# A gated retention and SGU layer on one core: u's projection in half-block products, the sums of the activations formed beside the retention, the mixing spread behind gate pairs

## The chip, the cores and the metric

The kernel runs on one core of one Trainium2 chip. The metric is the device time of one execution in microseconds, as the median of several runs. All inputs and the output are float32 in HBM; the kernel is written by hand in the Tile layer, which tracks dependences, allocates the buffers of its pools and orders each engine's instructions by a schedule made when the program is built.

## The reference, cut to what matters

SEQ = 512, D_MODEL = 1024, chunks of 128, 4 retention heads (dk 128, dv 256), 4 SGU groups, D_FF = 2816.

```
h    = rmsnorm(x, g_pre_mix)
q, k, v, g, u, sv, a_ret, a_sgu = split(h @ w_in)        # 512 512 1024 1024 1024 1024 1024 1024
y_ret = (layernorm(retention_fwd(q,k,v) + retention_bwd(q,k,v)) * silu(g)) @ w_ret_o
mixed = w_spatial (128 positions x 128, per group) @ layernorm(gelu(sv)) + b_spatial
y_sgu = (gelu(u) * mixed) @ w_sgu_o
x1   = x + rmsnorm((sigmoid(a_ret) * y_ret + sigmoid(a_sgu) * y_sgu) @ w_out, g_post_mix)
y    = x1 + rmsnorm(conv_gated_mlp(rmsnorm(x1, g_pre_ffn)), g_post_ffn)
```

## The kernel before, in words

**Products.** Every float32 matrix is split into a high part in float32r and the rest (`split`, L69 to L78: ScalarE copies the high part, VectorE subtracts), and a product is three matmuls, high x high, high x low, low x high (`mm3`, L164 to L166). Activations lie transposed, [channel, position], with 512 positions as the moving side; a weight block is 128 x 1024.

**Weights.** All weights are one array `wall` of 146 blocks. `w_get` (L150) hands out the next unit in order and prepares the following ones as far as slots allow: SyncE loads a block into one of 5 `raw` buffers (L106, pieces of block 0 at L119), and the split goes into 9 `w4` slots (two for a whole block, one for a half-block form). The order in which units are listed (L87 to L96) is the order of use.

**Order of the work.** (1) 18 matmuls on zeros (L201) while the first loads run; x transposed is loaded block by block (`load_x` L184, six `tmp` buffers), scaled by g_pre_mix and split (`x_low`, L193), and q and k are accumulated over the eight channel blocks in all 8 PSUM banks (L211, then `mm3`). (2) Decays, rotary tables, the iota tiles `dd` and `xx` (L303, in the big pool `blk` of 70 tiles) and their clips (L309). (3) For each of four heads the retention (`prep`, `k_rows`, `scores`, `states`, `values`), interleaved with `t_group` (L386 to L388), which projects v, sv and g. (4) `u` in eight whole blocks (`f_block`, L543), each followed by Gelu; between them `x_forms` (L558) loads x again and forms, on VectorE, the sums S1, S2, S4, and `x_form3` (L578) replaces the second half of xh and xl by a difference. (5) The spatial mixing of all eight channel blocks in one go (L674), evacuated by VectorE (L682, L690). (6) Eight gate pairs (`gated_pair`, L697), four with w_ret_o and four with w_sgu_o: a `Pair` (L589) computes two 128-channel blocks of a gate's projection in seven half-block products instead of eight (Strassen's scheme as Winograd arranged it), each of 12 matmuls of 256 columns (L603), on weight sums (T1 to T4, `w_form` L127) and activation sums; `part1` is four products, `part2` one, `part3` two with the sigmoid, and the two `f_block`s of the pair stand between part1 and part2 and between part2 and part3. (7) w_out (`Down`, L727), norms, the convolved MLP, w_down. Down takes all 8 PSUM banks.

**Names that the prediction uses.** T1, T2, T3, T4 and B11, B21, B22 are the seven weight forms. L637, L640 and L641 evacuate part3, L714 multiplies a block by its gate on VectorE, L715 adds the retention's share on GpSimd, L745 to L747 are Down's matmuls.

Of the kernel before, what the change touches and what calls it, by code (L numbers as in the profile page):

```python
# [24 lines left out]
DV = 256  # L25
EPS = 1e-6
NW = 146
GATE0, GATE1 = 40, 72
LOOK = 4
NBLK = 70  # L30
WARM = 18
# [9 lines left out]
def tile_block(ctx: ExitStack, tc, xT, x, wall, par, cs, decay, wsp, bsp, gpost, gffn, out):  # L41
# [25 lines left out]
    def const(n, shape):  # L67
        return sb.tile(list(shape), F32, tag=n, bufs=1, name=n)

    def copy(o, i):  # L70
        nc.scalar.activation(out=o, in_=i, func=AF.Copy)  # L71
# [12 lines left out]
    units = []  # L84
    i = 0
    while i < NW:
        if GATE0 <= i < GATE1:  # L87
            units += [("B11", i), ("B21", i), ("T1", i), ("T2", i), ("blk", i + 2), ("T3", i), ("blk", i + 3)]
            units += [("T4", i), ("B22", i)]
            i += 4  # L90
        else:
            units.append(("blk", i))
            i += 1
# [72 lines left out]
        nc.tensor.matmul(o, al, bh, start=False, stop=stop)  # L166


    part = const("part", [P, NPAR])
    nc.scalar.dma_start(part, par)  # L170

# [3 lines left out]
    nc.vector.memset(warm, 0.0)  # L175
    w16 = warm.bitcast(mybir.dt.bfloat16)
    copy(wact, warm[:, 0:16])

    def col(i):
        return part[:, i : i + 1]  # L180
# [116 lines left out]
    v.tensor_mul(sinr, sinr, rbc)  # L297


    (dp, dn), (xp, xn) = halves("dd"), halves("xx")  # L300

    def iota(o, pattern, base, mult):
        nc.gpsimd.iota(  # L303
            o, pattern=pattern, base=base, channel_multiplier=mult,
            allow_small_or_imprecise_dtypes=True,
        )

    def clip(o, i, op):
        v.tensor_scalar(out=o, in0=i, scalar1=0.0, scalar2=None, op0=op)  # L309

    iota(dp.rearrange("p (i n) -> p i n", i=2), [[-P, 2], [1, 256]], 0, -1)
    clip(dn, dp, ALU.min)
    clip(dp, dp, ALU.max)
    iota(xp, [[1, S]], -255, 0)
    iota(xn, [[1, S]], -256, 0)
    clip(xp, xp, ALU.max)
    clip(xn, xn, ALU.min)
    ze = const("ze", [P, NT])
# [175 lines left out]
    def sv_norm():  # L494
        for t in range(NT):
            for q in range(2):
                z = svz[t, q]
                v.tensor_scalar(
                    out=z, in0=z, scalar1=smv[:, t, 0:1], scalar2=srstd[:, t : t + 1],
                    op0=ALU.subtract, op1=ALU.mult,  # L500
                )
# [20 lines left out]
        transposed([o_sb[t, nh] for t in range(NT)], ogh, ogl)  # L522


    for h in range(H):
        gen = t_group()
        k_rows(h)
        sm = scores(h)
        acc = next(gen)
        st = states(h)  # L530
        next(gen)
        if h + 1 < H:
            prep(h + 1)
        values(h, sm, st)
        for _ in gen:
            pass
        (v_evac, sv_evac, sv_evac, g_evac)[h](acc, (1, 0, 1, 0)[h])
    for acc in t_group():
        pass
    sv_norm()  # L540
    g_evac(acc, 1)

    def f_block(ah, al, n):  # L543

        wh, wl = w_get()
        o = ps()
        for k in range(n):
            c = slice(k * P, (k + 1) * P)
            mm3(o, wh[:, c], wl[:, c], ah[k], al[k], k == 0, k == n - 1)
        return o  # L550

    T0, T1 = slice(0, 256), slice(256, 512)
    forms = {n: [] for n in ("S1", "S2", "S4")}

    def x_forms(k):  # L558

        a, b = tmp("xa"), tmp("xb")  # L560
        for t, j in ((a, k), (b, k + 4)):
            nc.sync.dma_start(t, xT[j])
            nc.scalar.activation(out=t, in_=t, func=AF.Copy, scale=col(PRE + j))
        s_ = tmp("xs")
        v.tensor_sub(s_[:, T0], a[:, T1], b[:, T1])
        v.tensor_sub(s_[:, T1], s_[:, T0], a[:, T0])
        h_, l_ = blk(F32R, "sh"), blk(F32R, "sl")
        split(h_, l_, s_)
        forms["S1"].append((h_[:, T0], l_[:, T0]))
        forms["S2"].append((h_[:, T1], l_[:, T1]))  # L570
        if k % 2 == 0:
            forms["s4"] = blk(F32R, "sh"), blk(F32R, "sl")
        h_, l_ = (t[:, (T0, T1)[k % 2]] for t in forms["s4"])
        v.tensor_add(s_[:, T0], b[:, T0], s_[:, T1])
        split(h_, l_, s_[:, T0])
        forms["S4"].append((h_, l_))

    def x_form3(k):  # L578

        a = tmp("xa")  # L580
        nc.sync.dma_start(a, xT[k])
        v.tensor_sub(a[:, T0], a[:, T0], a[:, T1])
        nc.scalar.activation(out=xh[k][:, T1], in_=a[:, T0], func=AF.Copy, scale=col(PRE + k))
        v.scalar_tensor_tensor(
            out=xl[k][:, T1], in0=a[:, T0], scalar=col(PRE + k), in1=as32(xh[k][:, T1]),
            op0=ALU.mult, op1=ALU.subtract,
        )

    class Pair:  # L589


        def __init__(self):
            self.b = [ps() for _ in range(3)]
            self.t = [tmp("p0"), tmp("p1")]

        def product(self, b, act, first):
            wh, wl = w_get()
            o = self.b[b][:, T0]
            for k in range(4):
                c = slice(k * P, (k + 1) * P)  # L600
                h_, l_ = act(k)
                for n, (w_, a_) in enumerate(((wh, h_), (wh, l_), (wl, h_))):
                    nc.tensor.matmul(  # L603
                        o, w_[:, c], a_, start=first and k == n == 0, stop=k == 3 and n == 2,
                        skip_group_check=True,
                    )
            return o
# [26 lines left out]
        def part3(self, func):  # L634
            c0, c1 = self.t
            o = self.product(0, self.x(4, T1), False)
            v.tensor_mul(c0[:, T1], o, rbc[:, T1])  # L637
            nc.scalar.activation(out=c0, in_=c0, func=func)
            o = self.product(2, self.s("S4"), False)
            v.tensor_sub(c1[:, T0], o, c1[:, T0])  # L640
            v.tensor_mul(c1, c1, rbc)  # L641
            nc.scalar.activation(out=c1, in_=c1, func=func)
            return c0, c1


    nc.sync.dma_start(wst, wsp)
# [3 lines left out]
    nc.tensor.matmul(rw, ones, wst, start=True, stop=True)  # L650
    rws = blk(n="rws")
    copy(rws, rw)
    uT = []
    for j in range(KD):
        o = f_block(xh, xl, KD)
        t = blk(n="u")
        v.tensor_mul(t, o, rbc)
        nc.scalar.activation(out=t, in_=t, func=AF.Gelu_apprx_tanh)
        uT.append(t)
        if j % 2:  # L660
            x_forms(j // 2)
    for k in range(4):
        x_form3(k)
    yh, yl = [], []
    for j in range(KD):
        gs = slice((j // 2) * P, (j // 2 + 1) * P)
        add = tmp("add", (P, P))
        v.scalar_tensor_tensor(
            out=add, in0=rws[:, gs], scalar=col(LNB + j), in1=bst[:, gs],
            op0=ALU.mult, op1=ALU.add,  # L670
        )
        o = ps()
        for t in range(NT):
            nc.tensor.matmul(  # L674
                o[:, t * P : (t + 1) * P],
                svz[t, j // 4][:, (j % 4) * P : (j % 4 + 1) * P],
                wst[:, gs],
                start=True,
                stop=True,
            )  # L680
        m = tmp("mix")
        v.scalar_tensor_tensor(  # L682
            out=m.rearrange("p (t q) -> p t q", t=NT),
            in0=o.rearrange("p (t q) -> p t q", t=NT),
            scalar=col(LNG + j),
            in1=add[:, None, :].to_broadcast([P, NT, P]),
            op0=ALU.mult,
            op1=ALU.add,
        )
        v.tensor_mul(uT[j], m, uT[j])  # L690
        h_, l_ = blk(F32R, "yh"), blk(F32R, "yl")
        split(h_, l_, uT[j])
        yh.append(h_)
        yl.append(l_)


    def gated_pair(ah, al):  # L697
        p = Pair()
        p.part1()
        o = [f_block(ah, al, KD)]  # L700
        p.part2()
# [296 lines left out]
```

## Time and profile before

| | |
|---|---|
| median of 3 runs | 857.89 us (857.30 to 858.48) |
| the profiled execution | 853.59 us, its span 851.8 us, granted TensorE clock 0.997 |
| busy in the span | PE 840.8, PEld 717.2, DVE 525.5, ACT 366.2, POOL 57.8 us |
| instructions | 10890, of them 4300 matmuls |
| HBM | 88.19 MB read, 2.10 MB written, 106 GB/s over the span |

The page's engines are PE (TensorE's matmuls), PEld (its weight loads), DVE (VectorE), ACT (ScalarE), POOL (GpSimd) and SP (SyncE, which issues nearly all loads here). A line number is that of the kernel before. "idle before, releaser" names what ended the time in which an engine stood still. Matmuls are pipelined, so a row's busy time of one is longer than the distance from one start to the next; the distance is what a stage's length shows. Times in microseconds count from the start of the span.

### The profile page before, as it was taken

The numbers are of one execution on the slowest core, as the hardware profiler recorded it, in microseconds if no ns is written. First come the engines' busy times: TensorE is split into PE (matmuls) and PEld (weight loads), VectorE is DVE, ScalarE is ACT, GpSimd is POOL, SyncE is SP. The second block draws the span as 40 slices with busy tenths as digits, with TensorE's granted clock in tenths as the row PEclk, the third lists the DMA queues.
The fourth block names the chain that finished last, engine by engine and source line by source line (L and its number), as shares of the span: only waits on it lengthen the run. The fifth ranks groups of instructions, "written<-read, shape, count | busy, mean of one in ns | idle before, by whom it ended". The sixth has DMA issues, their size and how long they took to land.

```text
span 851.8 us, 10890 instructions
## 1 busy us (share of the span) xinstructions
PE 840.8 (99%) x4300; PEld 717.2 (84%) x4300; DVE 525.5 (62%) x805; ACT 366.2 (43%) x575; POOL 57.8 (7%) x67
## 2 busy tenths in 40 slices
PE   8999999999999999999989999999999999999997
PEld 6888888888889899999978898888888888888885
DVE  6378888863669966667755766666666666322304
ACT  5534445543644533344534664444444444212201
POOL 0000000100000021123210100000000000000000
PEclk9999999999999999999999999999999999999998
DMA  9623212222332332323457032223222322222202
GB/s 337 232 91 115 80 53 75 75 86 95 129 107 67 128 121 99 100 98 101 131 168 246 1 103 99 96 98 99 100 98 99 99 99 98 91 93 90 74 1 99
DMA packets 28851, 90.99 MB, mean 107 GB/s; under 512 B 3264, under 2 KB 3904, under 8 KB 28800
## 3 DMA queue, kind: packets, MB, share of 16 engines
q1 hardware_dynamic: 27648, 87.96, 30.5%
q0 software_dynamic: 432, 1.32, 0.6%
q10 hardware_dynamic: 720, 1.02, 0.3%
q8 instruction: 33, 0.54, 0.3%
q14 instruction: 18, 0.15, 0.1%
HBM read 88.19 MB, written 2.10 MB: 106 GB/s over the span
## 4 chain that ended last, share of the span: by engine, by line
PE 97%; DVE 1%; DMA 1%; ACT 0%; POOL 0%; SPq 0%; issue 0%; POOLq 0%; DVEq 0%; ACTq 0%
PE ps L164 17%; PE ps L166 17%; PE ps L165 17%; PE ps L603 9%; PE ps L745 6%; PE ps L747 6%; PE ps L746 6%; PE ps L386 5%; PE ps L387 5%; PE ps L388 5%; PE ps L674 1%; DMA raw<-wall 1%; PE ps L211 1%; PE ps L511 0%; PE ps L807 0%; DVE wl L78 0%
## 5 line engine op out<-in xcount | busy, mean ns | idle before, releaser
L78 DVE TENSOR_TENSOR wl<-raw,wh 128x1024 fp32r<-128x1024 f32 (+1 forms) x139 | 162.1, 1177 | 188.0 <-PE ps L165 100.1
L71 ACT ACTIVATE wh<-raw 128x1024 fp32r<-128x1024 f32 (+2 forms) x141 | 137.2, 985 | 103.8 <-PE ps L747 40.9
L166 PE MATMUL ps<-h2h,wl 128*128 128x512 f32 (+1 forms) x384 | 142.3, 371 | 0.0
L165 PE MATMUL ps<-h2l,wh 128*128 128x512 f32 (+1 forms) x384 | 142.2, 371 | 0.0
L164 PE MATMUL ps<-h2h,wh 128*128 128x512 f32 (+1 forms) x384 | 142.2, 372 | 0.0
L166 PEld LDWEIGHTS ps<-h2h,wl 128*128 128x128 f32 x384 | 72.3, 188 | 12.6
L165 PEld LDWEIGHTS ps<-h2l,wh 128*128 128x128 f32 x384 | 72.3, 188 | 12.5
L164 PEld LDWEIGHTS ps<-h2h,wh 128*128 128x128 f32 x384 | 72.1, 188 | 12.5 <-ACT h2h L811 0.3
L386 PE MATMUL ps<-wh,xh 128*128 128x512 f32 x192 | 75.0, 391 | 0.0
L387 PE MATMUL ps<-wl,xh 128*128 128x512 f32 x192 | 74.9, 390 | 0.0
L388 PE MATMUL ps<-wh,xl 128*128 128x512 f32 x192 | 74.8, 390 | 0.0
L745 PE MATMUL ps<-wh,fh 128*128 128x512 f32 x176 | 68.5, 389 | 0.0
L746 PE MATMUL ps<-wl,fh 128*128 128x512 f32 x176 | 68.5, 389 | 0.0
L747 PE MATMUL ps<-wh,fl 128*128 128x512 f32 x176 | 68.5, 389 | 0.0
L854 ACT ACTIVATE cv<-ps,part 128x512 f32<-128x512 f32 x44 | 34.3, 780 | 76.3 <-PE ps L166 76.3
L71 ACT ACTIVATE wf<-raw 128x512 fp32r<-128x512 f32 x56 | 33.7, 625 | 59.4 <-PE ps L165 28.1
L603 PE MATMUL ps<-xh,wf 128*128 128x256 f32 x256 | 49.1, 281 | 0.0
L78 DVE TENSOR_TENSOR wf<-raw,wf 128x512 fp32r<-128x512 f32 x56 | 40.9, 742 | 12.0 <-ACT wf L71 11.5
L164 PE MATMUL ps<-xh,wh 128*128 128x512 f32 x120 | 46.8, 390 | 0.0
L166 PE MATMUL ps<-xh,wl 128*128 128x512 f32 x120 | 46.7, 389 | 0.0
L165 PE MATMUL ps<-xl,wh 128*128 128x512 f32 x120 | 46.7, 389 | 0.0
L388 PEld LDWEIGHTS ps<-wh,xl 128*128 128x128 f32 x192 | 36.1, 188 | 7.6
(232 smaller groups left out, 1545.6 us busy)
## 6 DMA issues: line engine op xcount, KB each, us to landing
raw<-wall SPq DMA_DIRECT2D x145, 512.0 KB, 3.3
x<-x SPq DMA_DIRECT2D x16, 256.0 KB, 6.0
xT<-xT SPq DMA_DIRECT2D x8, 256.0 KB, 5.6
xa<-xT SPq DMA_DIRECT2D x8, 256.0 KB, 2.9
xb<-xT SPq DMA_DIRECT2D x4, 256.0 KB, 3.6
out<-z SPq DMA_DIRECT2D x4, 256.0 KB, 2.0
out<-z ACTq DMA_DIRECT2D x3, 256.0 KB, 2.0
cs<-cs SPq DMA_DIRECT2D x2, 256.0 KB, 4.8
```

What stands on the lines that cost most here:

```text
L71: nc.scalar.activation(out=o, in_=i, func=AF.Copy)
L78: nc.vector.tensor_sub(lo, src, as32(hi))
L164: nc.tensor.matmul(o, ah, bh, start=start, stop=False)
L165: nc.tensor.matmul(o, ah, bl, start=False, stop=False)
L166: nc.tensor.matmul(o, al, bh, start=False, stop=stop)
L386: nc.tensor.matmul(acc[t], xh[k][:, c], wh[:, f], start=k == 0, stop=False)
L387: nc.tensor.matmul(acc[t], xh[k][:, c], wl[:, f], start=False, stop=False)
L388: nc.tensor.matmul(acc[t], xl[k][:, c], wh[:, f], start=False, stop=k == KD - 1)
L603: nc.tensor.matmul(o, w_[:, c], a_, start=first and k == n == 0, stop=k == 3 and n == 2, skip_group_check=True,)
L745: nc.tensor.matmul(o, ah, bh, start=k == 0, stop=False)
L746: nc.tensor.matmul(o, ah, bl, start=False, stop=False)
L747: nc.tensor.matmul(o, al, bh, start=False, stop=k == self.nk - 1)
```

## The change

- **u in pairs.** The eight blocks of u (32 to 39 of `wall`) become four `Pair`s with seven products each, with no whole block between them. The host lays u's weights out in quarters as it does those of the gates. part3 of a pair comes behind part1 of the next pair; the last one's behind part1 of the first gate pair.
- **Sums beside the retention.** `x_forms(h)` runs inside head h, in tiles of `blk` instead of `tmp`, its three sums on GpSimd (L536 of the changed kernel) instead of VectorE; the splits of its results follow one head later (`x_form_parts`). `x_form3` stays ahead of u's first pair; its difference is on GpSimd too, and its tile from `blk`.
- **The iota tiles** move from four `blk` tiles into two `raw` buffers that are allocated at the very top, ahead of the first weight block, and are filled there.
- **Mixing.** The eight channel blocks' mixing stands behind the first four gate pairs, two behind each.
- **Gate pairs.** part3 stands in the middle of the pair's second `f_block` (after four of its eight steps) instead of behind it; its two weight forms are taken ahead of the block.

```diff
-GATE0, GATE1 = 40, 72
+U0, GATE0, GATE1 = 32, 40, 72
...
-        if GATE0 <= i < GATE1:
-            units += [("B11", i), ("B21", i), ("T1", i), ("T2", i), ("blk", i + 2), ("T3", i), ("blk", i + 3)]
-            units += [("T4", i), ("B22", i)]
+        pair = [(f, i) for f in ("B11", "B21", "T1", "T2", "T3", "T4", "B22")]
+        if U0 <= i < GATE0:
+            units += pair
+            i += 2
+        elif GATE0 <= i < GATE1:
+            units += pair[:4] + [("blk", i + 2)] + pair[4:] + [("blk", i + 3)]
             i += 4
...
+    (dp, dn), (xp, xn) = ((t[:, :S], t[:, S:]) for t in (raw_tile(), raw_tile()))
+
     part = const("part", [P, NPAR])
     nc.scalar.dma_start(part, par)
...
+    iota(dp.rearrange("p (i n) -> p i n", i=2), [[-P, 2], [1, 256]], 0, -1)
+    iota(xp, [[1, S]], -255, 0)
+    iota(xn, [[1, S]], -256, 0)
...
-    (dp, dn), (xp, xn) = halves("dd"), halves("xx")
...
+    def x_forms(k):
+
+        a, b = blk(n="xa"), blk(n="xb")
+        for t, j in ((a, k), (b, k + 4)):
+            nc.sync.dma_start(t, xT[j])
+            nc.scalar.activation(out=t, in_=t, func=AF.Copy, scale=col(PRE + j))
+        s_ = blk(n="xs")
+        g_op(s_[:, T0], a[:, T1], b[:, T1], ALU.subtract)
+        g_op(s_[:, T1], s_[:, T0], a[:, T0], ALU.subtract)
+        g_op(b[:, T1], b[:, T0], s_[:, T1], ALU.add)
+        return s_, b[:, T1]
...
+    def x_form3(k):
+
+        a = blk(n="xa")
+        nc.sync.dma_start(a, xT[k])
+        g_op(a[:, T0], a[:, T0], a[:, T1], ALU.subtract)
+        nc.scalar.activation(out=xh[k][:, T1], in_=a[:, T0], func=AF.Copy, scale=col(PRE + k))
+        v.scalar_tensor_tensor(
+            out=xl[k][:, T1], in0=a[:, T0], scalar=col(PRE + k), in1=as32(xh[k][:, T1]),
+            op0=ALU.mult, op1=ALU.subtract,
+        )
...
         if h + 1 < H:
             prep(h + 1)
+        if h:
+            x_form_parts(h - 1, *xf)
+        xf = x_forms(h)
         values(h, sm, st)
...
-    def f_block(ah, al, n):
+    def f_block(ah, al, n, between=None):
...
+            if between and k == n // 2:
+                between()
...
-    uT = []
-    for j in range(KD):
-        o = f_block(xh, xl, KD)
-        t = blk(n="u")
-        v.tensor_mul(t, o, rbc)
-        nc.scalar.activation(out=t, in_=t, func=AF.Gelu_apprx_tanh)
-        uT.append(t)
-        if j % 2:
-            x_forms(j // 2)
     for k in range(4):
         x_form3(k)
+    uT, late = [], None
+    for j in range(KD // 2):
+        p = Pair(AF.Gelu_apprx_tanh, lambda: blk(n="u"))
+        p.part1()
+        if late:
+            late.part3()
+        p.part2()
+        late = p
+        uT += p.t
     yh, yl = [], []
-    for j in range(KD):
+
+    def mix(j):
...
-    def gated_pair(ah, al):
-        p = Pair()
+    def gated_pair(ah, al, late=None):
+        p = Pair(AF.Sigmoid, lambda: tmp("sig"))
         p.part1()
+        if late:
+            late.part3()
         o = [f_block(ah, al, KD)]
         p.part2()
-        o.append(f_block(ah, al, KD))
-        return zip(o, p.part3(AF.Sigmoid))
+        o.append(f_block(ah, al, KD, p.part3))
+        return zip(o, p.t)
...
     for j in range(KD // 2):
-        for o, t in gated_pair(ogh, ogl):
+        for o, t in gated_pair(ogh, ogl, late if j == 0 else None):
             b = blk(n="r")
             v.tensor_mul(b, o, t)
             r.append(b)
+        mix(2 * j)
+        mix(2 * j + 1)
...
-        _parts(u, 8, P),
+        _two(u).reshape(8, P, 1024),
```

More of the change, by code (lines that the diff above doesn't have):

```diff
@@ L177, in tile_block, with iota @@
     copy(wact, warm[:, 0:16])
+    def iota(o, pattern, base, mult):
+        nc.gpsimd.iota(
+            o, pattern=pattern, base=base, channel_multiplier=mult,
+            allow_small_or_imprecise_dtypes=True,
+        )
+    iota(dp.rearrange("p (i n) -> p i n", i=2), [[-P, 2], [1, 256]], 0, -1)
+    iota(xp, [[1, S]], -255, 0)
+    iota(xn, [[1, S]], -256, 0)
     def col(i):
@@ L297, in tile_block @@
     v.tensor_mul(sinr, sinr, rbc)
-    (dp, dn), (xp, xn) = halves("dd"), halves("xx")
[L302 to L306, printed above, removed]
     def clip(o, i, op):
         v.tensor_scalar(out=o, in0=i, scalar1=0.0, scalar2=None, op0=op)
-    iota(dp.rearrange("p (i n) -> p i n", i=2), [[-P, 2], [1, 256]], 0, -1)
     clip(dn, dp, ALU.min)
     clip(dp, dp, ALU.max)
-    iota(xp, [[1, S]], -255, 0)
-    iota(xn, [[1, S]], -256, 0)
     clip(xp, xp, ALU.max)
@@ L522, in g_evac, with g_op, x_form_parts @@
         transposed([o_sb[t, nh] for t in range(NT)], ogh, ogl)
+    T0, T1 = slice(0, 256), slice(256, 512)
+    forms = {n: [] for n in ("S1", "S2", "S4")}
+    def g_op(o, a, b, op):
+        nc.gpsimd.tensor_tensor(out=o, in0=a, in1=b, op=op)
+    def x_forms(k):
[8 more added lines that the diff above has]
+        return s_, b[:, T1]
+    def x_form_parts(k, s_, s4):
+        h_, l_ = blk(F32R, "sh"), blk(F32R, "sl")
+        split(h_, l_, s_)
+        forms["S1"].append((h_[:, T0], l_[:, T0]))
+        forms["S2"].append((h_[:, T1], l_[:, T1]))
+        if k % 2 == 0:
+            forms["s4"] = blk(F32R, "sh"), blk(F32R, "sl")
+        h_, l_ = (t[:, (T0, T1)[k % 2]] for t in forms["s4"])
+        split(h_, l_, s4)
+        forms["S4"].append((h_, l_))
+    def x_form3(k):
[6 more added lines that the diff above has]
+            op0=ALU.mult, op1=ALU.subtract,
+        )
     for h in range(H):
@@ L539, in tile_block @@
         pass
+    x_form_parts(3, *xf)
     sv_norm()
     g_evac(acc, 1)
-    def f_block(ah, al, n):
+    def f_block(ah, al, n, between=None):
         wh, wl = w_get()
@@ L550, in f_block, with __init__, product @@
         return o
[L555 to L587, printed above, removed]
     class Pair:
-        def __init__(self):
+        def __init__(self, func, alloc):
+            self.func, self.t = func, [alloc(), alloc()]
             self.b = [ps() for _ in range(3)]
-            self.t = [tmp("p0"), tmp("p1")]
-        def product(self, b, act, first):
-            wh, wl = w_get()
+        def product(self, b, act, first, w=None):
+            wh, wl = w or w_get()
             o = self.b[b][:, T0]
@@ L632, in part2, with part3 @@
             v.tensor_sub(c1[:, T1], self.b[2][:, T0], c1[:, T1])
-        def part3(self, func):
+            self.w = w_get(), w_get()
+        def part3(self):
             c0, c1 = self.t
-            o = self.product(0, self.x(4, T1), False)
+            o = self.product(0, self.x(4, T1), False, self.w[0])
             v.tensor_mul(c0[:, T1], o, rbc[:, T1])
-            nc.scalar.activation(out=c0, in_=c0, func=func)
-            o = self.product(2, self.s("S4"), False)
+            nc.scalar.activation(out=c0, in_=c0, func=self.func)
+            o = self.product(2, self.s("S4"), False, self.w[1])
             v.tensor_sub(c1[:, T0], o, c1[:, T0])
             v.tensor_mul(c1, c1, rbc)
-            nc.scalar.activation(out=c1, in_=c1, func=func)
-            return c0, c1
+            nc.scalar.activation(out=c1, in_=c1, func=self.func)
     nc.sync.dma_start(wst, wsp)
```

## The prediction

> **What bounds the kernel now.** I read the page first: the row of busy times, then the chain of work that ended last.
>
> ```profile
> PE 840.8 (99%) x4300; PEld 717.2 (84%) x4300; DVE 525.5 (62%) x805; ACT 366.2 (43%) x575; POOL 57.8 (7%) x67
> ...
> PE 97%; DVE 1%; DMA 1%; ACT 0%; POOL 0%; SPq 0%; issue 0%; POOLq 0%; DVEq 0%; ACTq 0%
> ```
>
> TensorE has work for 99% of 851.8 us and is 97% of the chain. So a change gains by taking matmul time away or by closing one of TensorE's few gaps, and it loses wherever it opens a gap. The view of waits, filtered to TensorE, lists the gaps.
>
> ```profile
> PE ps L745 <- DVE p L714: 2.3, 1, 2.3
> PE ps L211 <- ACT wh L71: 1.3, 2, 0.9
> ```
>
> One is in the middle (w_out waits for VectorE), the other at the start (the first projection waits for its weights). Stage lengths come from the chain in order of time (start, us, what).
>
> ```profile
> 217.70 0.23 PE ps L164
> ...
> 261.25 7.14 PE ps L674 x64
> ...
> 369.84 8.48 PE ps L603 x72
> ```
>
> u's projection runs from 217.70 to 261.25, which is 43.55 us for 192 matmuls of 512 columns (227 ns each). A matmul of 256 columns in the gates' pairs costs 8.48/72 = 118 ns. The mixing is 64 instructions in 7.14 us without a gap.
>
> **The change part by part.**
>
> *u in pairs.* Four pairs of seven products of twelve matmuls are 336 matmuls: 336 x 0.118 = 39.6 us in place of 43.55. **-4.0 us**, if TensorE is fed.
>
> *Mixing behind the gate pairs.* The same 64 instructions stand in four groups of 16, one behind each of the first four gate pairs. A gate pair in a window (length, then busy time of PE, PEld, DVE, ACT, POOL), and the mixing's evacuation among the groups by form:
>
> ```profile
> 307.40:328.20 20.80, 20.80 (x134) 18.89 (x133) 12.76 (x20) 8.29 (x14) 3.01 (x2) 1.00 0.31 102
> ```
>
> ```profile
> L682 DVE SCALAR_TENSOR_TENSOR mix<-ps,part,add 128x512 f32<-128x512 f32 x8 | 5.9, 741 | 0.0
> ```
>
> VectorE has 8.0 us free in each, and two mixes bring it two such operations, a multiply and a split each, some 4.2 us. **0**, hidden by the pair's matmuls; without that cover a group costs up to two evacuations, 1.5 us, and four of them 6.
>
> *part3 inside the second block.* Now the last pair is evacuated while four of the block's eight steps still run. The chain, where w_out begins before the change:
>
> ```profile
> 434.36 1.22 DVE wl L78
> ...
> 441.55 0.61 DVE p L714
> 442.20 0.50 PE ps L745
> ```
>
> TensorE wants all eight PSUM banks for w_out; the eighth is the last block's, which the second L714 frees only at 442.2, 7.8 us after the chain turns to the pair's evacuation, because its sigmoid comes after the block. Afterwards T4 ends 4.1 us before the block does (twelve matmuls of 118 ns and twelve of 227), so even the whole 7.8 us would free the bank 3.7 us after the block, and TensorE wants it 21 matmuls (4.8 us) after. The 2.3 us go; it takes a chain longer by 1.1 us to bring some back. What is late next is the last mh, wanted 60 matmuls (13.7 us) after the block. **-2.3 us**.
>
> *The iota tiles in two raw buffers, allocated first.* This is the part the diff hides. In the program order of the changed kernel, SyncE's queue starts with all eight xT loads and wst, and only then come the three pieces of the first weight block; before, one xT load stood ahead of them. The seventh xT load needs the first of six tmp buffers back, so SyncE waits for VectorE's first x_low, and the weights wait behind it. VectorE's order has all eight x_low and two clips ahead of the cast of the first piece. The timeline of before, the rows of the tile xT and its loads, and the row of the clips:
>
> ```profile
> 0.73 0.39 SPq L186 DMA_DIRECT2D xT<-xT  x1
> ...
> 1.04 3.78 PE L201 MATMUL ps<-warm 128*128 128x256 bf16 x18 [1.04 <-DVE warm L175]
> ...
> 4.09 0.72 ACT L188 ACTIVATE xh<-xT,part 128x512 fp32r<-128x512 f32 x1 [1.42 <-DMA part<-par]
> 4.29 0.23 DVE L120 CAST wh<-raw 128x128 fp32r<-128x128 f32 x1 [3.31 <-DMA raw<-wall]
> ...
> 4.84 0.75 DVE L194 SCALAR_TENSOR_TENSOR xl<-xT,part,xh 128x512 fp32r<-128x512 f32 x1 [0.32 <-ACT xh L188]
> ...
> 12.27 0.39 PE L164 MATMUL ps<-xh,wh 128*128 128x512 f32 x1
> ```
>
> ```profile
> L194 DVE SCALAR_TENSOR_TENSOR xl<-xT,part,xh x8: 744/748/752, 4.8 to 30.5; 128x512 fp32r<-128x512 f32 x8
> ...
> DMA to landing us min/median/max: 3.1/5.6/7.6
> ```
>
> ```profile
> L309 DVE TENSOR_SCALAR dd<-dd x2: 420/424/429, 52.1 to 52.6; 128x512 f32<-128x512 f32 x2
> ```
>
> From 4.84 VectorE has 8 x 0.75 + 2 x 0.42 + 0.23 = 7.1 us, so its cast ends at 11.9, or 11.1 if neighbours overlap as they do elsewhere; I take 11.5. The landing gives about the same: the first piece is issued near 7.2 (seventh x load after 5.6, eighth after 6.3, then wst) and lands at 10.4 by the shortest time of the row, 12.3 by a 5 us one. The 24 matmuls of k = 0 then need 24 x 0.227 = 5.45 us and end at 16.95; before, the next k starts at 12.27. That is **+4.7 us** (3.6 to 5.9 by the two landings).
>
> TensorE then stands still from 4.8 to 11.5. Windows of the end of before (stretch, length, busy per engine, granted clock, DMA) show what rest does to the clock:
>
> ```profile
> 845.00:846.00 1.00, 0.43 (x2) 0.01 (x1) 0.00 (x0) 0.47 (x1) 0.00 (x0) 1.00 0.00 0
> ...
> 847.00:848.00 1.00, 0.00 (x0) 0.00 (x0) 0.87 (x3) 0.00 (x0) 0.11 (x1) 0.77 0.00 0
> 848.00:849.00 1.00, 0.00 (x0) 0.00 (x0) 0.69 (x2) 0.00 (x0) 0.00 (x0) 0.50 0.23 88
> ```
>
> Two to three us after the last matmul the clock is half. Climbing out is seen in the warm-up row: 18 matmuls of 256 columns took 3.78 us, 210 ns each against 118 later, so 1.66 us were lost. Bounds are 0 (the clock holds) and the whole 3.78; I take the row's own, **+1.7 us**.
>
> The Trainium skill ("TensorE: Matmul & The Clock Gate", Part 1) says that the array drops to half clock after an idle window of about 3.4 us and climbs back only after about 3.4 us of sustained work, the windows running free. An estimate from that page alone is a loss of 1.7 to 3.4 us here, so the sum would be up to 1.7 us higher; the trace's rows agree with its lower end.
>
> *x_form3 on GpSimd.* The third-form halves of x must be there for T3 of pair 0, which TensorE reaches 64 matmuls (7.6 us) after u begins; its last reader stands 83 matmuls (9.8 us) after. In GpSimd's order the four subtractions stand behind T4 of pair 1, two before and two after T2 of pair 2. GpSimd's and VectorE's groups by form:
>
> ```profile
> L140 POOL TENSOR_TENSOR raw<-raw,raw 128x512 f32<-128x512 f32 x8 | 14.2, 1777 | 116.8 <-ACT sh L71 47.4 <-DMA raw<-wall 39.8 <-DVE raw L138 29.6
> ...
> L142 POOL TENSOR_TENSOR raw<-raw,raw 128x512 f32<-128x512 f32 x8 | 10.7, 1342 | 57.1 <-DVE wf L78 38.3 <-DMA raw<-wall 18.9
> ```
>
> ```profile
> L78 DVE TENSOR_TENSOR wf<-raw,wf 128x512 fp32r<-128x512 f32 x56 | 40.9, 742 | 12.0 <-ACT wf L71 11.5
> ...
> L139 DVE TENSOR_TENSOR raw<-raw,raw 128x512 f32<-128x512 f32 x8 | 9.9, 1233 | 0.1
> L641 DVE TENSOR_TENSOR p<-p,rbc 128x512 f32<-128x512 f32 x8 | 6.3, 790 | 0.0
> ...
> L138 DVE TENSOR_TENSOR raw<-raw 128x512 f32<-128x512 f32 x8 | 5.5, 683 | 0.0
> ...
> L640 DVE TENSOR_TENSOR p<-ps,p 128x256 f32<-128x256 f32 x8 | 3.4, 421 | 5.0 <-PE ps L603 5.0
> ```
>
> T4 of pair 1 waits for the split of T2, whose slot is freed when the second product ends (2.8 us) and which stands behind the transposes' copies: about 4.5 us. Then 1.3 (L142), two subtractions at half that, T2 at 1.8 (L140) and two more: 4.5 + 1.3 + 1.3 + 1.8 + 1.3 = 10.2, and ScalarE's and VectorE's halves, with a weight split between them, take until 11.9. TensorE stands for 11.9 - 9.8 = **+2.0 us**. Bounds: 0 (it is on time), 4.5 (a subtraction of 256 columns as slow as 512). No row shows one on GpSimd; half of L142 is nearest.
>
> Behind ScalarE's xh of that form stands its copy of pair 0's T2, which frees the bank that T3 accumulates into; it is late by less than the halves, so it adds nothing.
>
> *The sums beside the retention.* Per head they add to VectorE two splits (0.7 + 0.4) and to GpSimd three subtractions. One head before:
>
> ```profile
> 73.20:102.65 29.45, 29.45 (x163) 25.59 (x161) 25.64 (x44) 13.78 (x21) 1.21 (x2) 1.00 0.22 72
> ```
>
> GpSimd's work is not free to VectorE. The timeline of GpSimd, of VectorE where the two meet, and of VectorE where they don't:
>
> ```profile
> 437.38 1.29 POOL L715 TENSOR_TENSOR p<-p,r 128x512 f32<-128x512 f32 x1 [16.21 <-DVE p L714]
> ```
>
> ```profile
> 437.67 1.55 DVE L641 TENSOR_TENSOR p<-p,rbc 128x512 f32<-128x512 f32 x1
> ```
>
> ```profile
> 311.17 0.68 DVE L641 TENSOR_TENSOR p<-p,rbc 128x512 f32<-128x512 f32 x1
> ```
>
> A VectorE operation on two SBUF tensors begun beside GpSimd's ended 0.55 us after it: 1.55 us, not 0.68. The Trainium skill ("GPSIMD Engine Reference", 1. Specifications) says the same, that GpSimd shares its SBUF interface with such VectorE instructions; it speaks against moving sums to GpSimd while VectorE is full. So a head's VectorE work rises from 25.6 to 25.6 + 1.1 + some 2.0 = 28.7 of 29.45 us. I cost this at **0**: TensorE's next weight blocks are split up to three ahead, and scores and states are needed a block or more after they are made. If that cover is gone, it is up to 3.1 us in each of three heads. Three raw buffers for weights in place of five hold: a block lasts TensorE 5.5 us and takes 3.3 to land, by the page's row of its 145 loads.
>
> ```profile
> raw<-wall SPq DMA_DIRECT2D x145, 512.0 KB, 3.3
> ```
>
> *VectorE in u's stage.* A pair costs it 7 x 0.742 + 0.683 (the other sum, L138) + 1.233 + 5 x 0.42 + 0.79 = 10.0 us of busy rows (some 1 us of it overlap) against TensorE's 9.9. Its splits may lag, since the slots give a pair's weights seven products of lead; I cost it **0**, bounds 0 and 4 us.
>
> **Sum.** 4.7 + 1.7 - 4.0 + 2.0 - 2.3 = +2.1 us. The profiled execution (853.59 us, span 851.8) would become 855.7; it ran 4.3 us below the median of the runs shown, so I add the difference to the median: 857.89 + 2.1 = **860.0**. A difference under 0.2% (1.7 us) can't be told from none.
>
> **Rivals.**
> - *VectorE becomes the bound* in u's stage and the retention. For: 10.0 against 9.9 us, 28.7 of 29.45. Against: no gap in the retention before, seven products of lead. Half of the bounds, (9.3 + 4)/2 less the lag the lead absorbs (2), is +4.6: 864.6 us.
> - *The third-form halves are on time.* For: 64 matmuls, four of pair 1's among them, stand ahead of T3. Against: GpSimd's rows. 2.0 us less: 858.0, no change.
> - *The start is not lost* (the other side). If first pieces and their cast come as early as before, the 6.4 us vanish and 853.6 is left. It decides where the start costs under 2.6 us, a first matmul before 7.7. For: the loads ahead of the pieces are only 2.3 MB. Against: SyncE's and VectorE's orders, which are fixed when built.
>
> **How the numbers follow.** Forecast 46% (its own range 858.6 to 862.5, a quarter of it within 0.2%), VectorE 22%, halves on time 18% (a sixth of it slower), start not lost 14%. Faster 0.14; same 0.12 + 0.15 = 0.27; slower 0.34 + 0.22 + 0.03 = 0.59. The range reaches over both other cases on the slow side up to 865.5, a little past the first rival, and down to 855.8, the forecast with the start's lower bounds and the halves on time (3.6 + 0.5 - 4.0 - 2.3 = -2.2); below it lies most of the third rival, above it the first's end.
>
> **What would show it.** Right: the first projection matmul near 11.5 with a granted clock of 0.5 for some 3 us behind it; the next k 6 us later than 12.27; u's four pairs in 40 to 42 us with one wait of about 2 us on VectorE's or ScalarE's third-form half; no wait of w_out for L736's multiply. Wrong: a first matmul before 8 us, a clock that stays at 1.0, waits of TensorE spread over the heads or over pairs 1 to 3 of u, or u longer than 43.5 us.

## The result and the profile after

The changed kernel took 862.44 us (median of 7 runs, 860.78 to 864.96), the kernel before 857.25 (7 runs, 855.91 to 858.48): a ratio of 1.0062, 95% interval 1.0048 to 1.0077, so 5.2 us or 0.6% slower. The forecast was 860.0, its range 855.8 to 865.5.

The profiled execution took 862.76 us. Its page, busy times and the engines' shares of the chain:

```profile
PE 841.7 (98%) x4444; PEld 723.5 (84%) x4444; DVE 540.5 (63%) x833; ACT 377.3 (44%) x607; POOL 81.8 (9%) x91
...
PE 91%; DVE 3%; DMA 2%; issue 2%; ACT 1%; POOL 1%; SPq 0%; POOLq 0%; DVEq 0%; ACTq 0%
```

TensorE is busy no longer than before, but its share of the chain fell from 97% to 91%: other engines now set the end in several places. The view of waits, TensorE only (us in total, times, longest), names them:

```profile
PE ps L227 <- DVE wh L123: 6.6, 1, 6.6
PE ps L620 <- DVE xl L567: 1.6, 2, 1.0
PE ps L620 <- ACT u L71: 1.5, 2, 1.3
...
PE ps L768 <- DVE wl L78: 0.9, 1, 0.9
PE ps L169 <- DVE kz L78: 0.8, 1, 0.8
PE ps L767 <- DVE sig L736: 0.4, 1, 0.4
```

From the top: the start; in u the third-form halves, and ScalarE's copies that stand behind them; w_out's last resident weights; the fourth head's kz; the eighth PSUM bank. Before, only the last was there, at 2.3 us, and a shorter stop at the start, 1.3 us in two parts. The timeline shows the start:

```profile
0.72 5.68 SPq L202 DMA_DIRECT2D xT<-xT  x8
...
6.46 0.42 SPq L663 DMA_DIRECT2D wst<-wsp  x1
...
6.93 1.37 SPq L122 DMA_DIRECT2D raw<-wall  x3
...
11.34 0.22 DVE L123 CAST wh<-raw 128x128 fp32r<-128x128 f32 x1
...
11.70 3.75 PE L227 MATMUL ps<-xh,wh 128*128 128x512 f32 x8 [6.64 <-DVE wh L123]
...
15.25 2.86 PE L227 MATMUL ps<-xh,wl 128*128 128x512 f32 x8
...
17.95 1.99 PE L227 MATMUL ps<-xl,wh 128*128 128x512 f32 x8
...
19.77 0.39 PE L167 MATMUL ps<-xh,wh 128*128 128x512 f32 x1
```

All eight xT loads and wst are issued ahead of the first weight pieces, and the first product starts at 11.70. Its first eight matmuls take 3.55 us, the last eight 1.82: half speed to begin with. The next k (the first matmul of the second channel block) comes at 19.77, before at 12.27.

To see where the rest went I read from each trace's TensorE timeline when its stages begin, and took differences (us). "Before again" is a second profile of the unchanged kernel (e4, below); e7 and e12 are experiments:

| stage | before | before again (e4) | after | e7 | e12 |
|---|---|---|---|---|---|
| start, to the first head's transposes | 73.04 | 75.20 | 80.54 | 75.22 | 74.22 |
| four heads, to the first transposes behind them | 117.81 | 117.81 | 119.08 | 117.81 | 119.07 |
| to u's first product | 26.61 | 26.60 | 26.55 | 26.61 | 26.72 |
| u and all gate pairs, to w_out | 217.53 | 217.39 | 218.43 | 217.64 | 213.48 |
| w_out, to the first transposes behind it | 33.87 | 35.56 | 33.44 | 32.75 | 31.93 |
| from there to the last matmul | 376.19 | 376.18 | 376.18 | 376.19 | 376.19 |

Against the profile on which I worked, after loses 7.50 us at the start, 1.27 in the heads and 0.90 from u to w_out, and gains 0.43 in w_out: 9.2 us. The timed medians differ by 5.2 only. The second column explains that: the first profile of before (853.59 us) ran faster than any timed run of that kernel in this study (854.26 to 858.71). Against the second (857.28 us) after loses 5.34, 1.27 and 1.04 and gains 2.12, some 5.5 us in all, which is what the runs show.

### The profile page after: what moved, and what is told of

Its sections match the earlier page's. It is cut to its first block, busy times and chain, and to the rows that moved or that the text cites. A ratio compares the mean times of both kernels' runs of the same rounds, so it can differ in the third digit from the quotient of the medians.

```text
span 861.0 us, 11276 instructions
## 1 busy us (share of the span) xinstructions
PE 841.7 (98%) x4444; PEld 723.5 (84%) x4444; DVE 540.5 (63%) x833; ACT 377.3 (44%) x607; POOL 81.8 (9%) x91
## 4 chain that ended last, share of the span: by engine, by line
PE 91%; DVE 3%; DMA 2%; issue 2%; ACT 1%; POOL 1%; SPq 0%; POOLq 0%; DVEq 0%; ACTq 0%
PE ps L167 15%; PE ps L169 15%; PE ps L168 15%; PE ps L620 12%; PE ps L768 6%; PE ps L769 6%; PE ps L767 6%; PE ps L391 5%; PE ps L392 5%; PE ps L393 5%; DMA raw<-wall 1%; PE ps L227 1%; DVE wl L78 1%; PE ps L692 1%; ACT wh L71 1%
## 5 line engine op out<-in xcount | busy, mean ns | idle before, releaser
L78 DVE TENSOR_TENSOR wl<-raw,wh 128x1024 fp32r<-128x1024 f32 (+1 forms) x131 | 150.1, 1158 | 176.2 <-PE ps L168 84.8
L71 ACT ACTIVATE wh<-raw 128x1024 fp32r<-128x1024 f32 (+2 forms) x133 | 129.1, 982 | 99.4 <-PE ps L769 40.9
L71 ACT ACTIVATE wf<-raw 128x512 fp32r<-128x512 f32 x84 | 50.8, 626 | 83.4 <-issue 31.3
L78 DVE TENSOR_TENSOR wf<-raw,wf 128x512 fp32r<-128x512 f32 x84 | 63.8, 777 | 27.8 <-ACT wf L71 27.6
L620 PE MATMUL ps<-xh,wf 128*128 128x256 f32 x384 | 74.0, 283 | 1.3 <-ACT u L71 1.3
L620 PEld LDWEIGHTS ps<-xh,wf 128*128 128x128 f32 x384 | 61.4, 189 | 2.3 <-ACT u L71 1.5
L620 PE MATMUL ps<-sh,wf 128*128 128x256 f32 x288 | 55.7, 283 | 0.3 <-ACT u L71 0.2
L620 PE MATMUL ps<-xl,wf 128*128 128x256 f32 x192 | 54.3, 283 | 1.6 <-DVE xl L567 1.6
L620 PEld LDWEIGHTS ps<-sh,wf 128*128 128x128 f32 x288 | 46.5, 191 | 0.7 <-ACT u L71 0.7
```

The costliest lines, as they stand in the source:

```text
L78: nc.vector.tensor_sub(lo, src, as32(hi))
L620: nc.tensor.matmul(o, w_[:, c], a_, start=first and k == n == 0, stop=k == 3 and n == 2, skip_group_check=True,)
```

## The experiments

Ratios are to runs of before on the same chip. Differences in us to the changed kernel are between medians of different chips, on which the medians of before lie within 0.5 us of each other (857.06 to 857.52).

**e1, iota tiles in blocks.**

```diff
-    (dp, dn), (xp, xn) = ((t[:, :S], t[:, S:]) for t in (raw_tile(), raw_tile()))
+    (dp, dn), (xp, xn) = halves("dd"), halves("xx")
```

> The changed kernel with the iota tiles back in four half-width blocks, allocated at the same early place; nothing else differs. In its program order SyncE has one xT load ahead of the first weight pieces again, and VectorE casts piece 0 first. My theory (the accounting of the two traces): the start is worth 7.5 us of span, a first matmul at 4.9 instead of 11.70 and the next k at 12.3 instead of 19.77, so the span falls from 861.0 to about 853.5 and the time from 862.4 to about 855. Rival (the profiled execution of before was a lucky one, and an ordinary start of that order loses a few us as well): the next k near 16, time 858 to 860. If the scheduler's order, not the wait for weights, were without effect: 862.

Measured: 876.16 us, 1.0217 (1.0204 to 1.0230). All three expectations missed. The start gained only 0.9 us (first matmul at 10.97, now waiting for ScalarE's xh, which stands behind the casts of the weight pieces; SyncE issues the pieces at 1.16 here, as before). The rest is a surprise: most matmuls of 512 columns are 2 to 3% longer, to the end of the kernel. Windows of 100 us in the MLP, this run first, the changed kernel second:

```profile
600.00:700.00 100.00, 100.00 (x432) 81.16 (x431) 59.52 (x73) 42.06 (x54) 0.00 (x0) 1.00 0.28 95
```

```profile
600.00:700.00 100.00, 100.00 (x443) 82.81 (x442) 61.29 (x74) 43.75 (x56) 0.00 (x0) 1.00 0.30 98
```

432 matmuls against 443, TensorE busy throughout, granted clock 1.00 in both. e8 and e9 follow this up.

**e2, the subtractions of x_form3 on VectorE.**

```diff
-        g_op(a[:, T0], a[:, T0], a[:, T1], ALU.subtract)
+        v.tensor_sub(a[:, T0], a[:, T0], a[:, T1])
```

> The changed kernel with the four subtractions of x_form3 on VectorE instead of GpSimd. My theory: the waits of TensorE at u's third product (2.9 us) and the half clock behind them (1.7 us) come from GpSimd's queue, so both go: 4.6 us less span, first u pair without a wait over 0.3 us, time near 858. Rival: VectorE is the bound there and its four added subtractions (some 0.4 us each) delay the splits; the waits shrink to half at most, time 860 to 862.5.

Measured: 859.63 us, 1.0024 (1.0015 to 1.0032), 2.8 us less than the changed kernel. The stage from u to w_out went from 218.43 to 215.72. So GpSimd's queue held 2.7 us of the loss, not 4.6; the waits for xl are gone, while three for ScalarE's copies stay (2.0 us in all). Between theory and rival.

**e3, 76 warm-up matmuls in place of 18** (`WARM = 76`).

> The changed kernel with 76 warm-up matmuls instead of 18, so that TensorE works until about 11.7 us, when its first weights come; nothing else differs. My theory: the first 24 projection matmuls took 8.07 us instead of 5.45 because TensorE had rested for 6.6 us, although the granted clock in the windows stays at 1.00; warmed, they take about 5.5 and the time falls by 2.6 us to about 859.8. Rival: they are slow because the weights' pieces or the DMA traffic hold them; then nothing changes, 862.4.

Measured: 859.54 us, 1.0025 (1.0016 to 1.0035), 2.9 us less. The first product in this run:

```profile
12.04 1.17 PE L227 MATMUL ps<-xh,wh 128*128 128x512 f32 x4 [0.92 <-DVE wh L123]
...
17.62 0.39 PE L167 MATMUL ps<-xh,wh 128*128 128x512 f32 x1
```

Its 24 matmuls take 5.58 us instead of 8.07, so the rest ahead of them cost 2.5 us; the pieces were issued when they were in the changed kernel (6.94 us, there 6.93). The theory holds. (The stage of w_out is 1.2 us shorter here too, so not all of the 2.9 belongs to the start.)

**e4, the kernel before once more.**

> The kernel before, unchanged, for a second profile. Its first profiled execution took 853.6 us where the median of its timed runs is 857.3. If that profile was lucky, the second has a span near 855.5 and shows where some 3.7 us are lost in an ordinary execution: I look at the first projection's start and at the clock behind w_out's wait of 2.3 us. If profiles are always that much shorter than timed runs, its span is 851.8 again, and then the changed kernel's profile (862.8 against 862.4 timed) is the odd one.

Measured: 857.45 us, ratio 0.9997 (0.9989 to 1.0006), span 855.5. Two stages are longer than in the first profile, the start by 2.16 us and w_out by 1.69. Windows around both (length, busy PE, PEld, DVE, ACT, POOL, granted clock, DMA share, GB/s):

```profile
6.00:7.00 1.00, 0.00 (x0) 0.00 (x0) 0.00 (x0) 0.19 (x1) 0.00 (x0) 1.00 0.89 291
...
8.00:9.00 1.00, 1.00 (x4) 0.39 (x2) 0.08 (x1) 0.63 (x1) 0.00 (x0) 0.50 1.04 418
9.00:10.00 1.00, 1.00 (x4) 0.81 (x4) 0.61 (x1) 0.44 (x1) 0.00 (x0) 0.50 1.01 404
...
442.00:444.00 2.00, 0.00 (x0) 0.00 (x0) 1.74 (x3) 0.91 (x2) 0.00 (x0) 1.00 0.00 0
...
445.00:446.00 1.00, 1.00 (x4) 0.81 (x3) 0.00 (x0) 0.36 (x1) 1.00 (x2) 0.50 0.92 369
446.00:447.00 1.00, 1.00 (x4) 0.81 (x3) 0.70 (x2) 1.00 (x3) 0.65 (x2) 0.50 0.33 127
```

Both times TensorE stood still for 2.3 us and the clock fell to half behind it, four matmuls a microsecond. In the first profile the same wait in w_out (2.27 us) was followed by full speed. So the wait that the change removes costs not 2.3 us but, in this execution, 4.0 (2.3 and the 1.69 by which the stage is longer). At the start the first profile had 1.3 us of waits where this one has 2.3, so about 1 us of the 2.16 is a longer wait and only the rest the clock.

**e5, the iota tiles allocated and filled where before had them** (still raw tiles).

```diff
-    (dp, dn), (xp, xn) = ((t[:, :S], t[:, S:]) for t in (raw_tile(), raw_tile()))
...
-    iota(dp.rearrange("p (i n) -> p i n", i=2), [[-P, 2], [1, 256]], 0, -1)
-    iota(xp, [[1, S]], -255, 0)
-    iota(xn, [[1, S]], -256, 0)
...
     v.tensor_mul(sinr, sinr, rbc)
+    (dp, dn), (xp, xn) = ((t[:, :S], t[:, S:]) for t in (raw_tile(), raw_tile()))
+    iota(dp.rearrange("p (i n) -> p i n", i=2), [[-P, 2], [1, 256]], 0, -1)
+    iota(xp, [[1, S]], -255, 0)
+    iota(xn, [[1, S]], -256, 0)
     clip(dn, dp, ALU.min)
```

> The changed kernel with the two raw tiles of iota allocated and filled after the rope tables, where before had them; nothing else differs. SyncE's, ScalarE's and VectorE's orders then begin as those of before. My theory (the start costs what the traces show): the next k at 12.3 to 14.4 instead of 19.77, so 5.4 to 7.5 us less, time 855 to 857. Rival (two of five raw buffers gone from the first microsecond is what cost, not the orders): the same gain here too, but the projection then waits for weights where the iota tiles take their buffers, near 45 us. Rival (the start is bound by the DMAs in any order, as in the run with the tiles in blocks, whose next k came at 18.9): next k still near 19, time 861 to 862.

Measured: 856.68 us, 0.9990 (0.9981 to 1.0000), 5.8 us less than the changed kernel; next k at 13.87, start stage 74.65. The theory holds: the tiles' early place, allocation and fills together, cost the start, and without it the change makes no difference that can be measured. Which of the two it was is not shown, since both moved. No wait for weights appears where the tiles take their buffers.

**e6, e5 with e2's edit.**

> The run with iota late, and the four subtractions of x_form3 on VectorE as well. If the start and u's wait are separate losses, their gains add: 2.8 us less than the run with iota late alone, about 853 to 854, faster than before by 0.4 to 0.5%. Rival: VectorE, which then has nothing else late, becomes the bound in u; the gain shrinks to 1 us, 854.5 to 856.

Measured: 853.59 us, 0.9963 (0.9948 to 0.9978). The gains add (3.1 us beside e2's 2.8); the rival falls.

**e7, before with only part3 in the second block.**

```diff
-        o.append(f_block(ah, al, KD))
-        return zip(o, p.part3(AF.Sigmoid))
+        o.append(f_block(ah, al, KD, lambda: p.part3(AF.Sigmoid)))
+        return zip(o, p.t)
```

(with the unit order, `between` and `self.w` of the change)

> The kernel before, with part3 of the gates' pairs called inside the second block and the order of the weight units that goes with it; nothing else. The wait of 2.3 us in w_out goes, and with it the halved clock that followed it in the second profile of before. My theory: the time from w_out's first matmul to the first transposes of its end, 34.0 us in the first profile of before and 35.6 in the second, becomes 33.6 as in the changed kernel, because the last resident block's split comes late instead; time about 855.5. Rival (prediction's term and the clock both gained in full): 31.7 us, time near 853.3.

Measured: 854.54 us, 0.9967 (0.9950 to 0.9984). w_out takes 32.75 us, between the two expectations, and so does the time. Its waits end like those of the changed kernel; that for the bank is gone, that for the split of the last resident weights is there:

```profile
PE ps L211 <- ACT wh L71: 2.3, 2, 1.9
PE ps L201 <- DVE warm L175: 1.0, 1, 1.0
PE ps L749 <- DVE wl L78: 0.9, 1, 0.9
```

**e8, e1 with an unused tile of 896 bytes ahead** (`const("pad", [P, 224])`).

> The first run's kernel (iota tiles in blocks, allocated first, 876.2 us) with an unused tile of 896 bytes per partition allocated ahead of them. In that run every matmul, to the end of the kernel, took 2% longer (432 instead of 443 in 100 us, granted clock 1.00); its blocks lay 128 bytes past a multiple of 1024, those of before and of the changed kernel on multiples of 1024. My theory: the place of the blocks is the cause; on multiples of 1024 again, 443 matmuls in 100 us and a time near 860. Rival: the four blocks that the iota tiles hold through the retention, or the order, are the cause; still 874 to 877.

Measured: 875.05 us, 1.0205 (1.0188 to 1.0222). My theory fell as I had put it: the blocks' own place is not the cause, since they lay on multiples of 1024 again.

**e9, e1 with the blocks allocated behind part and wact.**

> The first run's kernel with the iota tiles in blocks, but allocated behind part and wact. The blocks then lie on multiples of 1024 bytes and the weight slots and raw tiles where they lie in before and in the changed kernel. In the two runs with 2% longer matmuls (876.2 and 875.1 us) blocks and slots stood 128 bytes apart in opposite ways: blocks moved by 128 in the first, raw and slots by 896 in the second. My theory: that distance between a matmul's two operands is the cause; here 443 matmuls in 100 us and a time of 858 to 861, the start still late. Rival: the four blocks held through the retention or the program's order are the cause; 874 to 877 and 432 matmuls.

Measured: 860.19 us, 1.0035 (1.0022 to 1.0048), and full speed:

```profile
600.00:700.00 100.00, 100.00 (x442) 82.79 (x442) 60.33 (x73) 42.67 (x55) 0.00 (x0) 1.00 0.29 95
```

The same four blocks are held through the retention, so the rival falls. Part's 832 bytes and wact's 64 stand ahead of the blocks again, 896 in all. By the sizes of the tiles (the traces show no addresses), e1 (blocks moved down) and e8 (slots moved up) share one thing: the weight slots begin 896 bytes further from the blocks than in e9. 896 is 3.5 x 256, the slots' pitch of 4352 is 17 x 256; that the remainder modulo 256 is what counts is a guess that no run here tests.

Whether the distance counts at all, the traces of e1 and e8 can tell. In w_down the first 18 weight blocks come from slots, the last four lie in blocks as the activations do. From one matmul to the next it takes on average 233 ns with weights from slots and 227 with weights in blocks, in e1 and in e8 alike; in the changed kernel and in e9 it takes 227 with both. In e1 both operands of the last four lie off their usual place, and nothing is lost. So it is not the blocks' own place, and the distance between the two operands fits all four kernels. The products' matmuls of 256 columns are not touched: their medians are 117 to 120 ns in all four.

**e10, e6 with the last head's three sums on VectorE.**

> The run with iota late and x_form3 on VectorE (853.6 us), and the last head's three sums of x_forms on VectorE too. My theory: in the changed kernel GpSimd has these three ahead of the rstd of the third head's norm, VectorE waits for that rstd with a weight split and the statistics of sv behind it, and so kz comes 1.27 us late in the fourth head; now it does not, and the time falls to about 852.3. Rival: the chain is as long on VectorE, whose order has the sums ahead of the norm; no change, 853.6.

Measured: 854.58 us, 0.9968 (0.9956 to 0.9980), no gain over e6; the four heads still take 119.09. I had moved the wrong three: the chain still runs through GpSimd's sums, which are those of the third head, k = 2. So this run says only that the last head's sums are not in it.

**e11, e10 with 40 warm-ups.**

> The same with 40 warm-up matmuls instead of 18, which last until about 7.4 us, when the second piece of the first weights comes. My theory: in ordinary executions of this order the first 24 matmuls are slow from a rest of 1 to 2.3 us, the next k comes near 14.4 instead of 12.9; warmed, 1.5 us less, about 850.8. Rival: the pieces' landing alone sets the start; no change against the run with 18.

Measured: 852.44 us, 0.9944 (0.9932 to 0.9956), 2.1 us less than e10, next k at 13.68 instead of 15.60. The theory holds.

**e12, e11 with the third forms early in tiles of their own.**

```diff
+        t = blk(F32R, "x3")
-        nc.scalar.activation(out=xh[k][:, T1], in_=a[:, T0], ...)
+        nc.scalar.activation(out=t[:, T0], in_=a[:, T0], ...)
...
+        forms["S3"].append((t[:, T0], t[:, T1]))
...
-            o = self.product(0, self.x(0, T1), False)
+            o = self.product(0, self.s("S3"), False)
```

(and the low part into t's other half; the calls stand ahead of the last transposes)

> The same again (40 warm-ups, last sums on VectorE) with the third-form halves in tiles of their own, made before the last transposes instead of over x's upper halves after them. My theory: what is left of u's waits (1.9 us in the run with iota late and x_form3 on VectorE, 2.2 us by its stage length) hangs on that late start, so they go: 2 us less than the run with 40 warm-ups, about 849. Rival: VectorE is the bound in u whatever comes first; the waits move to a later pair, within 0.5 us of the run with 40 warm-ups.

Measured: 850.15 us, 0.9920 (0.9907 to 0.9933): faster than both kernels. All waits of TensorE that are left:

```profile
PE ps L212 <- DVE warm L178: 1.0, 1, 1.0
PE ps L169 <- DVE kz L78: 0.8, 1, 0.8
PE ps L769 <- DVE wl L78: 0.4, 1, 0.4
PE ps L222 <- ACT wh L71: 0.3, 1, 0.3
```

None is in u. The stage from u to w_out fell to 213.48, 2.8 us below e11's 216.25: the rival (VectorE as the bound) falls.

## Why the prediction was right, and where its terms were not

The sign and the range held; the forecast was 2.4 us too low. That the time fell inside the range is in part luck: the two terms that were too small lie on the side that the range had left open for another reason (VectorE as the bound), and the start, forecast too dear, made up for part of them. By its own steps:

- **u in pairs, -4.0: right.** With u's waits gone (e12) its stage is 213.48 against 217.39 and 217.53, 3.9 to 4.05 us less. VectorE's 10.0 us a pair against TensorE's 9.9 cost nothing, as the zero there said, so the first rival had no ground in u.
- **Mixing, 0: right.** No row of TensorE's waits names it.
- **Start, first matmul at 11.5: right (11.70), and by the orders named.** The timeline above shows them, SyncE's and VectorE's; e5 undoes the loss by the place of the iota tiles alone. SyncE's order is not all that this place moves: in e1 and e9 it issues the pieces at 1.16, and the first matmul comes at 10.97 and 10.86 all the same, held by ScalarE's order. The bounds of +4.7 are not worked out alike: 10.4 gives 3.6 with no time for the cast, 12.3 gives 5.9 only with about 0.4 us for it. The range's lower end takes 0.5 us for the clock, whose bound had been 0.
- **Clock behind the start, +1.7: mechanism right, size off.** It measured 2.5 (e3). The sign that I had named for it, a granted clock of 0.5, did not show: a window over these matmuls reads 1.00.

```profile
12.70:13.70 1.00, 1.00 (x4) 0.81 (x3) 1.00 (x5) 0.21 (x1) 0.00 (x0) 1.00 0.99 406
18.70:19.70 1.00, 1.00 (x6) 0.84 (x5) 1.00 (x2) 0.78 (x3) 0.00 (x0) 1.00 0.85 274
```

  The count tells it: four matmuls touch the first microsecond, six the second, at the same granted clock. By the estimate from the Trainium skill ("TensorE: Matmul & The Clock Gate", Part 1) the loss would have been 1.7 to 3.4 us; the measured 2.5 lies inside. The idle window of about 3.4 us from which that estimate starts was not needed in e4, where stops of 2.3 us were followed by half clock.
- **x_form3 late, +2.0: mechanism right, size off; this is the term that missed most.** The loss is 218.43 - 213.48 = 5.0 us. GpSimd in that stretch:

```profile
230.85 1.28 POOL L145 TENSOR_TENSOR raw<-raw,raw 128x512 f32<-128x512 f32 x1 [12.15 <-DVE wf L78]
232.10 2.33 POOL L536 TENSOR_TENSOR xa<-xa 128x256 f32<-128x256 f32 x2
234.39 1.45 POOL L143 TENSOR_TENSOR raw<-raw,raw 128x512 f32<-128x512 f32 x1
235.80 1.78 POOL L536 TENSOR_TENSOR xa<-xa 128x256 f32<-128x256 f32 x2
```

  The order is the one that I worked through, and L145 begins 4.7 us after u, as estimated (4.5). But four subtractions took 4.1 us, not 2.7 (half of L142). Three waits of TensorE (1.33, 1.01 and 0.55 us) sum to 2.9 us, and I had not asked what they do to the clock:

```profile
239.00:240.00 1.00, 1.00 (x7) 1.00 (x6) 1.00 (x3) 0.00 (x0) 0.00 (x0) 0.50 0.75 164
240.00:241.00 1.00, 1.00 (x6) 1.00 (x6) 0.54 (x2) 0.61 (x1) 0.00 (x0) 0.50 1.02 373
241.00:242.00 1.00, 1.00 (x6) 1.00 (x6) 0.94 (x3) 0.93 (x3) 0.00 (x0) 0.50 0.86 344
```

  From 238.9 to 242.4 a matmul of 256 columns takes 213 ns instead of 118, some 1.5 us more. The copy of T2, which I had as adding nothing, ends the longest wait (1.33 us). 2.7 of the 5.0 were GpSimd's (e2); the rest went with the forms made early (e12 against e11). The waits and the half clock make up 4.4 of the 5.0; what is left fits a fourth wait of 0.2 us and the slower first matmul behind each stop.
- **Sums beside the retention, 0: wrong, +1.27 us**, and not where I bounded it. Heads one to three last 29.45 us each as before, so VectorE's fuller queue, and what GpSimd's work does to its operations, cost nothing there. VectorE was busy for 26.4 us of a head at most (the second), not the 28.7 that I had estimated. The chain of work from the third head into the fourth:

```profile
164.72 0.61 ACT xa L543
165.33 0.62 ACT xb L543
...
166.02 0.75 POOL xs L536
...
166.83 0.75 POOL xs L536
...
167.65 0.74 POOL xb L536
...
168.75 1.03 POOL orstd L249
...
170.13 1.05 DVE o L475 x3
171.19 1.13 DVE wl L78
172.32 2.38 DVE sst L492 x4
...
175.39 1.02 POOL srstd L249
...
176.90 0.70 DVE kz L78
```

  The failed step: I counted what the sums add to VectorE and not which small GpSimd operation stands behind them. orstd does; VectorE waits for it with a weight split and sv's statistics queued behind, a second such operation (srstd, sv's own) follows these, and the fourth head's kz comes late. Every kernel here with the sums loses this in the heads (119.08 or 119.09, e12 119.07; e1 and e8 aside, whose matmuls are longer), the three profiles without them (before twice, and e7) do not; that the queue behind orstd is the cause is read from the chain and was not shown by an undo, since e10 moved other sums.
- **part3 in the block, -2.3: the wait went (0.35 us left), the size depends on the reference.** w_out gained 0.43 us against the first profile and 2.12 against the second. What is late next is not the last mh but the split of the last resident weight block (0.92 us on its wl), and the stall's price in an ordinary execution includes the half clock behind it (e4).
- **The reference.** I worked against one profiled execution and added its 4.3 us below the median as if that were the same everywhere. It sat in the two stages that the change touches, the start and w_out, where the clock had happened to hold and the wait at the start was shorter. Against the second profile the start lost 5.34 us, not the forecast 6.4. Against it the errors are 3.0 us too little for the halves, 1.3 too little for the sums and 1.1 too much for the start, 3.2 in all; the medians differ by 5.2 where I forecast 2.1.
- **"The start is not lost" priced at 853.6:** e5 is that case and took 856.7. The price left the forms' 2.0 in place, where e5's stage from u to w_out (219.65) carries 6.2.

## What to carry to other kernels

Tiles that are merely allocated and filled earlier can reorder every queue at the start: read the program order of each engine, not the diff. Price a stall of TensorE with the half clock that may follow it, and take a second profile of the kernel before when its profiled time lies outside its timed runs. When work is moved to a nearly idle engine, list the small operations in that engine's queue that others wait for.

## What the runs showed of the hardware

Stops of TensorE of 2.3 us at the start and in w_out (e4), and in u of the changed kernel three of 1.33, 1.01 and 0.55 us within 5 us, were each followed by some 3.4 us at half clock. (At e4's start, for one, the granted clock was 0.92, 0.50, 0.50, 0.50 and 0.88 in the five windows from 7 to 12 us.) A stop of 2.27 us in another execution of the same kernel was followed by full speed. What decides between the two is not shown. The timed runs of before spread by some 4 us; that such stops are the reason is not shown either.

How far apart a matmul's two operands lie can cost 2% of a kernel: with the weight slots 896 bytes further from the blocks (by the tiles' sizes), it takes 875 to 876 us where it takes 860 otherwise (e1, e8, e9), with nothing in the granted clock or in the waits to tell. Only matmuls of 512 columns whose weights come from slots are longer, 233 ns instead of 227. Whether the matmul's own two reads, or an engine's traffic beside them, make it so was not tried.
